# Products of the substitution in other buffers, more turns for the projections, four HGRN tiles moved forward, and all low parts of weights on DVE

## The chip, the cores and the metric

The kernel runs on one core of a Trainium2 chip. The metric is the time of one execution in microseconds (us), taken on the device; the median of several runs counts. The engines of the core are named as in the profile: PE (matrix products; its weight loads are PEld), DVE (vector), ACT (scalar, activation functions), POOL (general) and SP, which issues most of the transfers.

## The reference

One decoder layer on 512 tokens of width 2048, in float32. Two groups of heads share one input projection, and a mixer of single-neuron experts (PEER) follows.

```
xn = rmsnorm(x);  proj = xn @ w_in            # 57 column tiles of 128
o_a = hgrn2(a_q, a_f, a_i)                    # 8 heads: S_t = diag(f_t) S_{t-1} + (1-f_t) v_t ; o_t = S_t^T q_t
qkv = silu(causal_conv(b_q|b_k|b_v));  q, k l2-normalised
o_b = gated_delta(q, k, v, beta, g)           # 8 heads on 4 q/k pairs; chunkwise:
      M = I + strict_lower(kb k^T * L);  u, w = M^-1 (v beta), M^-1 (kb exp(g))
h = x + concat(gated_norm(o_a), gated_norm(o_b)) @ w_out
hn = rmsnorm(h);  scores = hn @ w_query @ sub_keys;  top-16 of each, top-16 of sums -> experts, gates
y_t = sum_e gate_e * gelu(u_e . hn_t) * v_e   # 16384 experts
out = rmsnorm(h + y)
```

## The kernel before

**Weights.** Every weight goes through `wunit`: SP loads a raw tile of 128x1024 (`wr`), ACT casts it to the short format (`wh`, L100), and the difference of the two, the low part (`wl`, L102), is made by POOL, or by DVE where the call says so. Each of the three has three buffers. A projection step (`mm3`, L239 to L241) is then three products: high weight with high and low activation, low weight with high activation. Sixteen steps fill one column tile. 114 units belong to the input projection, 32 to the output projection, 32 to PEER's queries: their low parts are on POOL. The 512 units of the expert tables have theirs on DVE.

**Front.** The input is normalised and split into high and low (`front`, L742). Then the projection stream (`proj_steps`, L210) and the heads run interleaved: a chain of a head is a generator, and at each of its `yield`s the loop `run` (L253) gives the stream a number of turns, 1.8 in the GDN pairs (RATE_B) and 5.0 in the HGRN heads (RATE_A). A turn is one step, three products. The stream stops short where two tiles of the coming kind are still unused. `jobs` (L722) lists the column tiles in order: the gates, then what the four pairs need, then forget, query, value and gate tile of each HGRN head.

**A pair.** `gdn_pair` (L402) makes the keys' Gram matrix (L420), two matrices to be inverted, and sends their 32x32 diagonal blocks through memory. `substitute` (L482) inverts these blocks row by row on DVE: 31 steps, each a product into a buffer `m` (L498) and a sum into `T_` (L500), with a `yield` after every fourth. The results return through memory, and `inverse` (L512) joins them to 128x128 by small products on PE (L527, L533, L542), whose copies go to the buffers `iTN` and `iY`. Beside the substitution the queries are normalised (`unit_q`, `l2n`): a square on ACT into a buffer `t_sq` (L376), a product with ones on PE (L380). `m` is taken from the same two `t_sq` buffers. L442 is the product of q and k; the chains of the two heads follow.

**A head.** `hgrn_head` (L605) needs its forget and query tile first, then goes through seven levels, each some products on PE (L624, L631) and some work on DVE (L587, L638, L639), then states (L653) and output (L666).

**Then** the output projection (`wout_steps`), PEER's scores with top-16 on DVE (`scores`, `top16`, L956 to L970), and the experts, which take the rest of the time.

**Order.** A scheduler puts the instructions of each engine in an order when the kernel is built; each engine works off its own queue in that order. So the places below are those of the built program.

Of the kernel before, what the change touches and what calls it, by code (L numbers as in the profile page):

```python
# [33 lines left out]
IB = 32  # L34
# [43 lines left out]
class Kernel:  # L78
# [12 lines left out]
        return (pool or self.fp).tile(list(shape), dt, tag=tag, name=self.nm(tag), bufs=bufs)  # L91


    def wunit(self, src, raw=False, eng=None):
        nc, wp = self.nc, self.wp
        full = raw
        raw = wp.tile([P, 8, P], F32, tag="wr", name=self.nm("wr"))
        nc.sync.dma_start(raw, src)
        hi = wp.tile([P, 8, P], F32R, tag="wh", name=self.nm("wh"))
        nc.scalar.copy(hi, raw)  # L100
        lo = wp.tile([P, 8, P], F32R, tag="wl", name=self.nm("wl"))
        (eng or nc.gpsimd).tensor_tensor(lo, raw, hi.bitcast(F32), op=ALU.subtract)  # L102
        return (raw, hi, lo) if full else (hi, lo)

    def linear(self, src, halves, xh, xl, ps):
# [376 lines left out]
    def substitute(self):  # L482


        nc = self.nc
        TT = self.TT
        nb = self.ft("iN", (P, IB, IB))
        T_ = self.ft("iT", (P, 8, IB))
        nc.sync.dma_start(T_, self.a["eye"])
        yield  # L490
        for g in range(IG):
            nc.sync.dma_start(nb[g * NX:(g + 1) * NX], self.nd.rearrange("j h c s t -> (j h c) s t"))
        for _ in range(WAIT):
            yield
        for s in range(IB - 1):
            w = IB - 1 - s
            m = self.ft("t_sq", bufs=2)[:, 0:8 * IB].rearrange("p (j i) -> p j i", j=8)[:, :, 0:w]
            nc.vector.tensor_tensor(m, nb[:, s:s + 1, s + 1:].to_broadcast([P, 8, w]),  # L498
                                    T_[:, :, s:s + 1].to_broadcast([P, 8, w]), op=ALU.mult)
            nc.vector.tensor_tensor(T_[:, :, s + 1:], T_[:, :, s + 1:], m, op=ALU.add)  # L500
            if s % 4 == 3:
                yield
        for g in range(IG):
            nc.sync.dma_start(self.td.rearrange("j h c s t -> (j h c) s t")[:, 8 * g:8 * g + 8],
                              T_[g * NX:(g + 1) * NX])
        for j in range(P // IB):
            sl = slice(j * IB, (j + 1) * IB)
            nc.sync.dma_start(TT[sl, :, :, sl], self.td[j].rearrange("h c s t -> s h c t"))
        for _ in range(WAIT):
            yield  # L510
# [211 lines left out]
    def jobs(self):  # L722

        key = lambda j: (36 + j, lambda ps: self.conv_silu(ps, 4 + j, "gk"), "k")
        out = [(56, self.gates, "gates")]
        for j in range(4):
            if j == 0:
# [2 lines left out]
            for h in (2 * j, 2 * j + 1):  # L730
                if j < 3 and h % 2:
                    out.append(key(j + 1))
                out.append((40 + h, lambda ps, h=h: self.conv_silu(ps, 8 + h, "gv"), "v"))
                out.append((48 + h, self.gate, "u"))
        for h in range(8):
            out.append((8 + h, lambda ps, h=h: self.forget(ps, h), "f"))
            out.append((h, lambda ps: self.keep(ps, "hQ"), "r"))
            out.append((16 + h, lambda ps: self.keep(ps, "gv"), "v"))
            out.append((24 + h, self.gate, "u"))
        return out  # L740
# [366 lines left out]
    def u_steps(self, et):  # L1107
# [1 line left out]
        nc = self.nc  # L1109
        ps = self.pt("lin")[:, 0:TD]  # L1110
        for h in (0, 1):
            hi, lo = self.wunit(self.a["u"][et][h], eng=nc.vector)
            for k in range(8):
                self.mm3(ps, hi[:, k], lo[:, k], 8 * h + k, k + h == 0, 8 * h + k == KT - 1)
            if h == 0:
# [35 lines left out]
    def v_chunk(self, g, dc, w, last):  # L1151

        nc = self.nc
        wh, wl = w
        hi, lo = self.wunit(self.a["v"][g, dc].rearrange("p (x y) -> p x y", x=8), eng=nc.vector)
        hv, lv = (x.rearrange("p (e z) n -> p e (z n)", e=4) for x in (hi, lo))
        for dd in range(2):
            dt = 2 * dc + dd
# [187 lines left out]
```

## Time and profile before

| | |
|---|---|
| median of 3 runs | 3533.93 us (3527.35 to 3548.31) |
| profiled execution | 3537.38 us, span 3534.2 us |
| granted PE clock, mean | 0.966 |
| busy: PE, DVE, ACT, POOL | 3323.9, 2760.3, 1206.8, 878.8 us |
| start to the gates (0 to 65 us) | PE busy 42.3 us, clock 0.91 |
| four GDN pairs (65 to 541 us) | PE busy 428.3 of 475.6 us, clock 0.88 |
| HGRN heads (541 to 951 us) | PE busy 403.5 of 410.0 us, clock 1.00 |
| output projection and scores (951 to 1353 us) | PE busy 384.8 of 402.2 us |
| the rest (experts) | PE busy 2065.1 of 2181 us |

In rows of the profile, `wl<-wr,wh` means that tile wl is written from wr and wh, L102 is the line, and `x54` the number of instructions. A time in brackets at a row's end, as `[6.94 <-ACT t_sq L376]`, is how long the engine had been idle before, and what ended that. In a table of waits the numbers are the total in us, how many, and the longest. A window row gives its bounds and length in us, the busy times, then the granted clock, the busy share of the transfer engines and GB/s.

### The profile page before, as it was taken

What the parts mean: (1) busy time and instruction counts of PE and PEld (TensorE: products, weight loads), DVE (VectorE), ACT (ScalarE), POOL (GpSimd) and SP (SyncE); (2) the same over time, 40 slices, a digit from 0 to 9 for tenths busy, and PEclk for the clock granted to TensorE, in tenths of its full rate; (3) what the DMA queues carried; (4) which work ended last, traced back from release to release, by engine and by line L of the source; (5) the groups of instructions that cost most, each with busy time, mean ns of one, the idle gap of its engine ahead of it and who ended that gap; (6) DMA issues with size and microseconds to landing.
All of it is one profiled execution on the core that took longest, in us unless ns stands there. A gap on an engine that the chain in (4) does not pass through costs nothing.

```text
span 3534.2 us, 49832 instructions
## 1 busy us (share of the span) xinstructions
PE 3323.9 (94%) x19740; PEld 3085.3 (87%) x19740; DVE 2760.3 (78%) x4095; ACT 1206.8 (34%) x1499; POOL 878.8 (25%) x533
## 2 busy tenths in 40 slices
PE   7889899999999997898999799999999998999997
PEld 5667678888788896898989799999999998999997
DVE  7675654444534679998999799998999998999966
ACT  5333433322332212343435233332333334333334
POOL 4232223333354231011121222222222222111100
PEclk9899989999999998999999999999999999999999
DMA  4232222222442223677788899999999999999963
GB/s 147 76 96 88 83 64 81 78 81 78 130 130 85 71 66 120 209 293 292 277 318 294 316 346 375 370 368 355 358 360 365 372 366 333 349 322 335 332 183 111
DMA packets 238028, 801.63 MB, mean 227 GB/s; under 512 B 30202, under 2 KB 99066, under 8 KB 194978
## 3 DMA queue, kind: packets, MB, share of 16 engines
q1 hardware_dynamic: 191714, 462.88, 37.9%
q0 software_dynamic: 46080, 335.56, 25.2%
q8 instruction: 154, 2.52, 0.3%
q14 instruction: 80, 0.66, 0.1%
HBM read 754.50 MB, written 43.86 MB: 226 GB/s over the span
## 4 chain that ended last, share of the span: by engine, by line
PE 51%; DVE 19%; issue 14%; DMA 12%; POOL 2%; ACT 1%; SPq 0%; DVEq 0%; POOLq 0%; ACTq 0%
PE lin L239 8%; PE lin L241 7%; PE lin L240 7%; DMA row<-vn,eidx 3%; DVE wl L102 3%; DMA wr<-u 3%; PE g L1165 2%; PE g L1164 2%; PE g L1163 2%; POOL row L1205 2%; PE lin L1165 2%; PE lin L1164 2%; PE lin L1163 2%; DVE row L1218 2%; DMA wr<-v 1%
## 5 line engine op out<-in xcount | busy, mean ns | idle before, releaser
L100 ACT CAST wh<-wr 128x1024 fp32r<-128x1024 f32 x690 | 724.5, 1050 | 1708.8 <-DMA wr<-v 402.3
L241 PE MATMUL lin<-yh,wl 128*128 128x352 f32 x2048 | 673.0, 329 | 68.5 <-DVE wl L102 68.2
L102 DVE TENSOR_TENSOR wl<-wr,wh 128x1024 fp32r<-128x1024 f32 x512 | 623.3, 1219 | 81.6 <-ACT wh L100 80.3
L239 PE MATMUL lin<-yh,wh 128*128 128x352 f32 x2048 | 673.3, 329 | 9.5 <-ACT wh L100 9.5
L240 PE MATMUL lin<-yl,wh 128*128 128x352 f32 x2048 | 668.0, 326 | 0.0
L102 POOL TENSOR_TENSOR wl<-wr,wh 128x1024 fp32r<-128x1024 f32 x178 | 432.8, 2432 | 872.8 <-ACT wh L100 809.8
L241 PEld LDWEIGHTS lin<-yh,wl 128*128 128x128 f32 x2048 | 391.3, 191 | 78.8 <-DVE wl L102 78.4
L1205 POOL DMA_INDIRECT row<-un,eidx x160 | 212.4, 1328 | 809.7 <-DVE row L1218 626.2
L239 PEld LDWEIGHTS lin<-yh,wh 128*128 128x128 f32 x2048 | 391.7, 191 | 11.3 <-ACT wh L100 11.3
L1205 POOL DMA_INDIRECT row<-vn,eidx x160 | 201.2, 1258 | 782.8 <-DVE y_nat L1231 416.0
L240 PEld LDWEIGHTS lin<-yl,wh 128*128 128x128 f32 x2048 | 391.1, 191 | 0.0
L239 PE MATMUL lin<-xh,wh 128*128 128x512 f32 x912 | 381.4, 418 | 8.9 <-ACT xh L766 8.8
L1165 PE MATMUL g<-wgh,wl 128*128 128x352 f32 x1188 | 384.9, 324 | 3.5 <-DVE wl L102 3.3
L1164 PE MATMUL g<-wgl,wh 128*128 128x352 f32 x1188 | 385.4, 324 | 0.0
L1163 PE MATMUL g<-wgh,wh 128*128 128x352 f32 x1188 | 382.4, 322 | 2.3 <-ACT wh L100 2.3
L240 PE MATMUL lin<-xl,wh 128*128 128x512 f32 x912 | 375.5, 412 | 2.5 <-DVE xl L767 2.3
L241 PE MATMUL lin<-xh,wl 128*128 128x512 f32 x912 | 373.0, 409 | 4.4 <-POOL wl L102 4.4
L1231 DVE SCALAR_TENSOR_TENSOR y_nat<-row,ww,y_nat 128x2048 f32<-128x2048 f32 x128 | 300.3, 2346 | 11.1 <-DMA row<-vn,eidx 10.7
L1218 DVE SCALAR_TENSOR_TENSOR row<-row,hn_nat 128x2048 f32<-128x2048 f32 x128 | 292.1, 2284 | 1.7 <-DMA row<-un,eidx 1.5
L1165 PEld LDWEIGHTS g<-wgh,wl 128*128 128x128 f32 x1188 | 223.3, 188 | 5.5 <-DVE wl L102 5.4
L1163 PEld LDWEIGHTS g<-wgh,wh 128*128 128x128 f32 x1188 | 223.5, 188 | 2.6 <-ACT wh L100 2.6
L1164 PEld LDWEIGHTS g<-wgl,wh 128*128 128x128 f32 x1188 | 223.2, 188 | 0.0
(348 smaller groups left out, 5879.5 us busy)
## 6 DMA issues: line engine op xcount, KB each, us to landing
wr<-u SPq DMA_DIRECT2D x256, 512.0 KB, 6.2
wr<-v SPq DMA_DIRECT2D x256, 512.0 KB, 6.7
wr<-wi SPq DMA_DIRECT2D x114, 512.0 KB, 3.6
gd<-st SPq DMA_DIRECT2D x11, 2048.0 KB, 13.6
gm<-gd SPq DMA_DIRECT2D x32, 704.0 KB, 9.3
wr<-wo SPq DMA_DIRECT2D x32, 512.0 KB, 3.6
wr<-wq SPq DMA_DIRECT2D x32, 512.0 KB, 3.5
hidd<-hid SPq DMA_DIRECT2D x64, 176.0 KB, 5.2
```

The costliest lines, as they stand in the source:

```text
L100: nc.scalar.copy(hi, raw)
L102: (eng or nc.gpsimd).tensor_tensor(lo, raw, hi.bitcast(F32), op=ALU.subtract)
L239: mm(ps, hi, self.xh[:, k], start=first, stop=False)
L240: mm(ps, hi, self.xl[:, k], start=False, stop=False)
L241: mm(ps, lo, self.xh[:, k], start=False, stop=last)
L1163: nc.tensor.matmul(ps, hv[:, e, sl], wh[:, e], start=(e == 0), stop=False)
L1164: nc.tensor.matmul(ps, hv[:, e, sl], wl[:, e], start=False, stop=False)
L1165: nc.tensor.matmul(ps, lv[:, e, sl], wh[:, e], start=False, stop=(e == 3))
L1205: ins = nc.gpsimd.indirect_dma_start(out=r, out_offset=None, in_=self.a[tab], in_offset=bass.IndirectOffsetOnAxis(ap=idx, axis=0))
L1218: nc.vector.scalar_tensor_tensor(r, r, 1.0, hn, op0=ALU.mult, op1=ALU.mult, accum_out=ww[:, i:i + 1])
L1231: nc.vector.scalar_tensor_tensor(y, r, ww[:, i:i + 1], y, op0=ALU.mult, op1=ALU.add)
```

## The change

Four edits. The products `m` of the substitution go in turn to the buffers `iTN` and `iY`, which the inverse uses later. The substitution yields after every second step in place of every fourth. Four tiles of the heads 0 and 1 (forget 0, query 0, forget 1, query 1) are taken into the list of jobs among the tiles of the four pairs. And `wunit` makes every low part on DVE, 178 of them that were on POOL.

```diff
--- before.py
+++ after.py
@@ -91,7 +91,7 @@
         return (pool or self.fp).tile(list(shape), dt, tag=tag, name=self.nm(tag), bufs=bufs)
 
 
-    def wunit(self, src, raw=False, eng=None):
+    def wunit(self, src, raw=False):
         nc, wp = self.nc, self.wp
         full = raw
         raw = wp.tile([P, 8, P], F32, tag="wr", name=self.nm("wr"))
@@ -99,7 +99,7 @@
         hi = wp.tile([P, 8, P], F32R, tag="wh", name=self.nm("wh"))
         nc.scalar.copy(hi, raw)
         lo = wp.tile([P, 8, P], F32R, tag="wl", name=self.nm("wl"))
-        (eng or nc.gpsimd).tensor_tensor(lo, raw, hi.bitcast(F32), op=ALU.subtract)
+        nc.vector.tensor_tensor(lo, raw, hi.bitcast(F32), op=ALU.subtract)
         return (raw, hi, lo) if full else (hi, lo)
 
     def linear(self, src, halves, xh, xl, ps):
@@ -494,11 +494,11 @@
             yield
         for s in range(IB - 1):
             w = IB - 1 - s
-            m = self.ft("t_sq", bufs=2)[:, 0:8 * IB].rearrange("p (j i) -> p j i", j=8)[:, :, 0:w]
+            m = self.ft(("iTN", "iY")[s % 2])[:, 0:8 * IB].rearrange("p (j i) -> p j i", j=8)[:, :, 0:w]
             nc.vector.tensor_tensor(m, nb[:, s:s + 1, s + 1:].to_broadcast([P, 8, w]),
                                     T_[:, :, s:s + 1].to_broadcast([P, 8, w]), op=ALU.mult)
             nc.vector.tensor_tensor(T_[:, :, s + 1:], T_[:, :, s + 1:], m, op=ALU.add)
-            if s % 4 == 3:
+            if s % 2:
                 yield
         for g in range(IG):
             nc.sync.dma_start(self.td.rearrange("j h c s t -> (j h c) s t")[:, 8 * g:8 * g + 8],
@@ -722,6 +722,8 @@
     def jobs(self):
 
         key = lambda j: (36 + j, lambda ps: self.conv_silu(ps, 4 + j, "gk"), "k")
+        forget = lambda h: (8 + h, lambda ps: self.forget(ps, h), "f")
+        query = lambda h: (h, lambda ps: self.keep(ps, "hQ"), "r")
         out = [(56, self.gates, "gates")]
         for j in range(4):
             if j == 0:
@@ -732,9 +734,11 @@
                     out.append(key(j + 1))
                 out.append((40 + h, lambda ps, h=h: self.conv_silu(ps, 8 + h, "gv"), "v"))
                 out.append((48 + h, self.gate, "u"))
+
+            out.append(forget(j // 2) if j % 2 == 0 else query(j // 2))
         for h in range(8):
-            out.append((8 + h, lambda ps, h=h: self.forget(ps, h), "f"))
-            out.append((h, lambda ps: self.keep(ps, "hQ"), "r"))
+            if h >= 2:
+                out += [forget(h), query(h)]
             out.append((16 + h, lambda ps: self.keep(ps, "gv"), "v"))
             out.append((24 + h, self.gate, "u"))
         return out
@@ -1109,7 +1113,7 @@
         nc = self.nc
         ps = self.pt("lin")[:, 0:TD]
         for h in (0, 1):
-            hi, lo = self.wunit(self.a["u"][et][h], eng=nc.vector)
+            hi, lo = self.wunit(self.a["u"][et][h])
             for k in range(8):
                 self.mm3(ps, hi[:, k], lo[:, k], 8 * h + k, k + h == 0, 8 * h + k == KT - 1)
             if h == 0:
@@ -1152,7 +1156,7 @@
 
         nc = self.nc
         wh, wl = w
-        hi, lo = self.wunit(self.a["v"][g, dc].rearrange("p (x y) -> p x y", x=8), eng=nc.vector)
+        hi, lo = self.wunit(self.a["v"][g, dc].rearrange("p (x y) -> p x y", x=8))
         hv, lv = (x.rearrange("p (e z) n -> p e (z n)", e=4) for x in (hi, lo))
         for dd in range(2):
             dt = 2 * dc + dd
```

The scheduler answers with another order. On DVE, where the substitution of pair 0 begins, before; in the names, `t_sq` is a product's buffer, `iT` the sum, `gv` and `t_u` tiles of the stream:

```order
L364 SCALAR_TENSOR_TENSOR t_y_586<-pad_583,sm,t_y_586 128x512 x3
L359 MEMSET pad_1033 128x3
L369 SCALAR_TENSOR_TENSOR gv_593<-t_th_591,t_y_586 128x512
L498 TENSOR_TENSOR t_sq_605<-iN_531,iT_532 128x8x31
L500 TENSOR_TENSOR iT_532<-iT_532,t_sq_605 128x8x31
L498 TENSOR_TENSOR t_sq_608<-iN_531,iT_532 128x8x30
```

and after:

```order
L383 SCALAR_TENSOR_TENSOR gq_507<-gq_507,t_r_690 128x512
L245 TENSOR_TENSOR t_u_714<-lin_595,rstd_a 128x512
L102 TENSOR_TENSOR wl_849<-wr_845,wh_847 128x1024
L498 TENSOR_TENSOR iTN_605<-iN_531,iT_532 128x8x31
L444 TENSOR_TENSOR geg_389<-gq_507,geg_389 128x512
L500 TENSOR_TENSOR iT_532<-iT_532,iTN_605 128x8x31
L285 SCALAR_TENSOR_TENSOR t_u_714<-t_th_713,t_u_714 128x512
L498 TENSOR_TENSOR iY_608<-iN_531,iT_532 128x8x30
```

A low part now stands directly ahead of the first step, the products alternate between two other buffers, and the normalised query (L383) is finished before the substitution begins.

On ACT, around the square of pair 0's query (`t_sq<-gq`), before:

```order
L100 CAST wh_977<-wr_975 128x1024
L100 CAST wh_1052<-wr_1050 128x1024
L367 ACTIVATE t_th_899<-t_y_894 128x512
L376 ACTIVATE t_sq_686<-gq_507 128x512
L100 CAST wh_1098<-wr_1096 128x1024
```

and after:

```order
L150 ACT_TABLE_LOAD
L376 ACTIVATE t_sq_656<-gq_507 128x512
L100 CAST wh_727<-wr_725 128x1024
L367 ACT_TABLE_LOAD
L367 ACTIVATE t_th_591<-t_y_586 128x512
```

The square stood behind the tanh of the tile that DVE works off during the substitution (the key tile, `t_y_894`); now it stands ahead of the tanh of the tile before (`t_y_586`), which is worked off before the substitution begins.

On PE, at the states of the first HGRN head (`lin` is the stream's tile), before:

```order
L241 MATMUL lin_4233<-xh,wl_4238 128x512
L653 MATMUL g_4275<-gTn_4253,gN_4246 128x128 x3
L239 MATMUL lin_4233<-xh,wh_4236 128x512
L240 MATMUL lin_4233<-xl,wh_4236 128x512
L241 MATMUL lin_4233<-xh,wl_4238 128x512
L239 MATMUL lin_4233<-xh,wh_4290 128x512
```

and after:

```order
L239 MATMUL lin_4454<-xh,wh_4497 128x512
L653 MATMUL g_4313<-gTn_4306,gN_4299 128x128 x3
L666 MATMUL o_4323<-gL_4133,gTn_4306 128x128 x2
L240 MATMUL lin_4454<-xl,wh_4497 128x512
L241 MATMUL lin_4454<-xh,wl_4499 128x512
```

Between the states and the head's output stood 15 products of the stream; now none does.

## The prediction

> **What bounds the kernel now.** I read the busy times by stage first, then the waits of the stage that the change touches, then the order of events around each wait. The rows of stages give, for a stretch in us, its length and the busy time of PE, PE's weight loads, DVE, ACT and POOL, then the granted clock.
>
> ```profile
> 65.20:540.80 475.60, 428.29 (x2197) 335.15 (x2196) 293.25 (x598) 182.06 (x251) 131.39 (x54) 0.88 0.28 83
> 540.80:639.20 98.40, 96.88 (x533) 81.05 (x532) 44.91 (x87) 28.53 (x33) 32.60 (x14) 1.00 0.26 81
> 1075.00:1353.00 278.00, 261.98 (x1624) 250.82 (x1622) 176.69 (x772) 55.19 (x67) 92.11 (x42) 0.98 0.24 76
> ```
>
> The first row is the four GDN pairs: PE is idle for 47.3 of 475.6 us and its clock is 0.88. The second is HGRN heads 0 and 1: PE is full, at full clock, and DVE works less than half the time. The third is the query scores, where DVE is at 177 of 278 us. So PE's stream of projection products (lines 239 to 241, "projections" below) sets the time of the front, except in the pairs, where something else holds PE up. Within a pair two stretches matter: from the product of the keys (L420) to the first transpose of the inverse (L527), here called the window, and from there to the product of q and k (L442), here the block.
>
> ```profile
> 73.60:136.40 62.80, 54.25 (x230) 43.50 (x229) 57.76 (x104) 27.55 (x31) 22.56 (x10) 0.92 0.33 92
> 424.70:489.30 64.60, 55.57 (x234) 44.40 (x232) 44.57 (x91) 25.01 (x29) 23.41 (x10) 0.92 0.31 92
> sum 256.40, PE 217.40 PEld 174.08 DVE 200.80 ACT 97.85 POOL 92.26; mean PE 54.35 PEld 43.52 DVE 50.20 ACT 24.46 POOL 23.06
> ```
> ```profile
> 136.40:156.00 19.60, 19.60 (x142) 13.91 (x142) 3.25 (x11) 4.29 (x8) 3.98 (x2) 0.55 0.09 28
> 257.80:278.70 20.90, 20.90 (x142) 14.84 (x142) 2.56 (x10) 3.65 (x7) 2.36 (x1) 0.50 0.15 50
> 379.50:392.80 13.30, 13.30 (x148) 9.74 (x148) 8.05 (x17) 6.53 (x10) 2.36 (x1) 1.00 0.30 91
> 489.30:509.90 20.60, 20.60 (x143) 14.53 (x143) 2.56 (x10) 3.65 (x7) 2.39 (x2) 0.51 0.09 27
> ```
>
> The first and the last of the four windows, their sum, and the four blocks. The windows hold 39 us of PE's idle time. Three of the four blocks ran at about half the clock. What PE waits for, in total, times and longest:
>
> ```profile
> PE g L380 <- ACT t_sq L376: 30.2, 4, 9.1
> ACT t_sq L376 <- DVE iT L500: 11.9, 2, 6.1
> PE g L527 <- DMA gT<-gTd: 6.5, 3, 3.1
> ```
> ```profile
> 117.61 0.63 ACT L367 ACTIVATE t_th<-t_y 128x512 f32<-128x512 f32 x1 [10.04 <-DVE t_y L364]
> 118.14 0.61 ACT L376 ACTIVATE t_sq<-gq 128x512 f32<-128x512 f32 x1
> 118.81 2.08 PE L380 MATMUL g<-t_sq,fc 128*128 128x512 f32 x2 [6.94 <-ACT t_sq L376]
> ```
>
> Once per pair PE stops at the norm of q (L380), 30.2 us in all. It waits for the square on ACT (L376). In two pairs that square waits for a t_sq buffer that the substitution's products hold (L500); in the pair shown it stands on ACT behind a tanh that waits for a convolution that DVE works off between the substitution's steps. Then DVE and POOL:
>
> ```profile
> 95.80 0.41 DVE L500 TENSOR_TENSOR iT<-iT,t_sq 128x240 f32<-128x240 f32 x1
> 97.17 2.25 DVE L500 TENSOR_TENSOR iT<-iT,t_sq 128x232 f32<-128x232 f32 x1
> 96.77 2.40 POOL L102 TENSOR_TENSOR wl<-wr,wh 128x1024 fp32r<-128x1024 f32 x1 [2.17 <-ACT wh L100]
> ```
> ```profile
> L102 DVE TENSOR_TENSOR wl<-wr,wh x512: 1194/1218/1281, 1347.2 to 3504.0; 128x1024 fp32r<-128x1024 f32 x171
> L102 POOL TENSOR_TENSOR wl<-wr,wh x54: 2337/2392/2912, 73.6 to 540.0; 128x1024 fp32r<-128x1024 f32 x54
> ```
> ```profile
> L100 ACT CAST wh<-wr 128x1024 fp32r<-128x1024 f32 x690 | 724.5, 1050 | 1708.8 <-DMA wr<-v 402.3
> ```
>
> A smaller step of the substitution took 2.25 us in place of 0.41 because a low part ran on POOL, and it ended just behind it. The low part itself takes 2.39 us (median) on POOL and 1.22 us on DVE; the cast ahead of it takes 1.05 us on ACT.
>
> **Prices.** A projection costs 0.228 us: twelve starts in 2.74 us.
>
> ```profile
> 821.33 0.40 PE L241 MATMUL lin<-xh,wl 128*128 128x512 f32 x1
> ...
> 824.07 0.40 PE L241 MATMUL lin<-xh,wl 128*128 128x512 f32 x1
> ```
>
> **The turns and the four tiles.** The order of instructions gives the number of projections in each stretch. Windows: 217, 218, 209, 220 before (864), 258, 254, 254, 235 after (1001). Blocks: 93 and 93. Rest of the pairs: 336 and 363. Heads 0 and 1: 326 and 156; from there the counts are alike. So 170 projections, 38.8 us of PE's work, leave the heads, where PE is full; 137 of them go into the windows and 27 into the rest (6 more before the pairs). Those in the rest I price in full, +6 us. Whether those in the windows are free depends on how long a window becomes.
>
> **The windows.** Three pieces, from the rows of the substitution:
>
> ```profile
> 92.38:128.84 36.46, 15.41 (x31) 0.86 0.24 75
> sum 139.94, DVE 48.83; mean DVE 12.21
> sum 139.94, DVE 56.96; mean DVE 14.24
> L498 DVE TENSOR_TENSOR t_sq<-iN,iT x124: 162/292/2561, 92.4 to 479.2; 128x248 f32<-128x248 f32 x4, 128x240 f32<-128x240 f32 x4, 128x232 f32<-128x232 f32 x4, 128x224 f32<-128x224 f32 x4
> 77.41 2.33 DVE L364 SCALAR_TENSOR_TENSOR t_y<-pad,sm,t_y 128x512 f32<-128x512 f32 x3
> ```
>
> The first row is pair 0's substitution with its L498 instructions; the two sums are L498's and L500's busy time in all four, 105.8 us in 139.9 us. At L498's median, which I take for L500 too, the 248 instructions would need 72.5 us: POOL stretches them by 33 us. Without POOL that is gone, but 23 low parts now stand between the steps (28 us), and the tails of two and a half more tiles (two more convolutions, 2.33 us and three single passes each, 8.6 us in all). So the substitutions grow by some 3 us. Ahead of them, pair 0's window takes 18.8 us (92.4 less 73.6), all four 84.6; after, the last low part ahead of the first step needs PE to be 69, 65, 65 and 70 projections past the keys, which with L380 (2.1 us), a cast and a low part for each comes to 79 us: -6. Behind them the way through memory to L527 stays at 7.6 us, -1 in pair 3. Sum, with the overlap of neighbouring instructions on DVE rounded off, -5: 251 us. Bounds: PE's own work there, 1001 x 0.228 + 4 x 2.1 = 237 us (-19), and +12, if each low part in the windows holds DVE up for half a us more.
>
> That the square no longer waits follows from its place: ahead of the substitution, in buffers that nothing else holds. The products themselves cost what they did: iTN and iY are next written by the inverse's copies (L528, L537), behind the last step. The 30 us of L380 are therefore not a term of their own; the 137 projections (31 us) fill them. What is late next is L527: after, the last low part of a substitution needs PE within 45 projections of L527 (10.3 us), while cast, low part, last steps and the way through memory need about 11 us. PE will again wait for L527, by about 1 us.
>
> **The blocks.** At full clock such a block takes 13.3 us with 27 projections, 12.2 with 22; the three slow ones lost 61.1 - 36.6 = 24.5 us. They stood behind the three waits for L527; the fourth, with no wait, ran at 1.00. With waits of about 1 us, between none and the shortest that slowed a block, I take half: -12 (0 to -24.5).
> By the Trainium skill (TensorE: Matmul & The Clock Gate, section "Why this matters for your kernels") the clock falls back after an idle gap of about 3 us or more. The row of the three waits differs: 6.5 us in all, the longest 3.1, and each followed by a slow block, so shorter waits did it too; the measurement decides. By the rule shorter waits would save nothing here, and the sum would end 12 us higher.
>
> **The start.**
>
> ```profile
> 33.49 11.61 DVE L776 TENSOR_TENSOR t_acc<-t_acc,t_sq 128x512 f32<-128x512 f32 x7
> 36.24 8.32 POOL L102 TENSOR_TENSOR wl<-wr,wh 128x1024 fp32r<-128x1024 f32 x3
> 46.13 2.07 PE L137 MATMUL o<-t_sq,fc 128*128 128x512 f32 x2 [3.44 <-DVE t_sq L779]
> ```
>
> Three low parts on POOL stretch the seven last sums of squares, on which the first norm waits. After, these three stand on DVE behind the sums, but three others ahead of them (3.7 us). I take -5 of 8.3 us (0 to -9).
>
> **Heads 0 and 1.** PE's work falls to 98.4 - 38.8 = 59.6 us. A level needs its chain through DVE:
>
> ```profile
> 656.45 1.00 PE L624 MATMUL g<-hQ,hK 128*128 128x64 f32 x8
> 657.49 0.44 DVE L587 COPY_PREDICATED gL<-mk,g 128x256 f32<-128x256 uint8 x1 [3.01 <-PE g L624]
> 658.16 0.42 DVE L639 TENSOR_TENSOR hK<-hK,hf 128x256 f32<-128x256 f32 x1
> ```
>
> That is 2.1 us from a level's products to what the next ones need; with the 1.00 us of the products and 6 to 9 projections between (1.4 to 2.1 us), PE is just covered. Behind L653 no projection is left ahead of L666. New idle time +5 (0 to +14): -34 in all.
>
> **Output projection and scores.** 64 low parts add 78 us to DVE, which has room (177 of 278 us in the scores).
>
> ```profile
> PE g L959 <- DVE t_y L956: 15.8, 7, 2.4
> ```
>
> PE already waits for an odd tile's scores, behind the top-16 work. The next tile's low part now stands directly behind that instruction: at most 1.2 us more for 8 tiles, less what POOL stretched. +2 (-8 to +10).
>
> Sum: -5 -5 -12 +6 -34 +2 = -48. The profiled execution took 3537.4 us (its span and 3.2 around it), 3.5 above the median of 3533.9: the median becomes 3486. The PEER stages keep their instructions; SP issues as many loads, each now released by DVE's reading of the raw weights where it was POOL's; POOL keeps its squares at the start, its 16 scalings and its gathers.
>
> **Rivals.**
> First, PE sets the windows: DVE stays ahead, they shrink to 237 us (-14 more) and L527 finds its data, so that all blocks run at full clock (-12 more): 3460. For it: DVE overlaps successive instructions, which my sum ignores; pair 2 had no wait. Against: the 45 projections above.
> Second, the low parts hold DVE. DVE takes its queue in order, so a low part that waits for its cast holds every step behind it.
>
> ```profile
>   ACT wh L100: 286.7, 45
> ```
>
> POOL waited for casts 45 times in the pairs, 6.4 us each, at nobody's cost. If each of 61 low parts there costs 0.4 us of PE's time, 3510. Against: the order sets each where its cast is due.
> By the Trainium skill (TensorE: Matmul & The Clock Gate, its opening table) the queues of ScalarE and VectorE are strict FIFO; the trace agrees, L376 above starting only as L367 ends.
> Third, the turns are only moved: heads 0 and 1, bare of projections, take as long as before, because their chain is what lasts: 3486 + 34 = 3520, about no change. Against: the 2.1 us of a level.
> Fourth, slower: in the scores PE runs out of low parts behind each odd tile's 44 DVE instructions, two thirds of a tile pair's 22 us (177 by 8), so some 15 us. Were all of that, less the 2.2 us it waits now, a wait on each of the 8 odd tiles, 3486 + 8 x 12.8 = 3588; it decides from 8 us a tile on. Against: both units of the odd tile stand ahead of that run.
>
> **Chances.** My sum 0.54 (3470 to 3502), first rival 0.20, second 0.16, third 0.06, fourth 0.04. About 0.5% (18 us) is what a measurement of this kernel tells from no change. Faster by more: 0.54 + 0.20 + most of the second, 0.85; within: 0.11; slower 0.04. The range reaches from beyond the first rival to the third: 3452 to 3519.
>
> **What would show it.** No wait of PE for L376; DVE steps of the substitution without any near 2.4 us; 1001 projections in windows of about 251 us; PE at L527 waiting about 1 us and the clock of the blocks; heads 0 and 1 in some 65 us; scores at 278 us. I am wrong if low parts on DVE show long waits for ACT, or if PE in the pairs waits for them.

## The result, and the profile after

The changed kernel takes 3431.53 us (median of 4 runs, 3425.67 to 3437.62), against 3533.8 us before: a ratio of 0.9715, interval 0.9686 to 0.9745. On a second chip it took 3439.49 against 3526.95 us: 0.9747, 0.9721 to 0.9773. The forecast was 3486, range 3452 to 3519: the sign was right, the gain was twice what was forecast, and the time lies below the range. The profiled execution took 3437.6 us, its span is 3435.8.

The three stages that the prediction began with (bounds and length in us, then busy PE, weight loads, DVE, ACT, POOL, then the granted clock): the pairs, heads 0 and 1, the scores. The prediction's row for the scores, 278.0 us from 1075, also held 39 us of the output projection; the last row here is the kernel before from the first product of the scores on, to be set beside the third.

```profile
55.74:478.30 422.56, 420.07 (x2362) 336.60 (x2362) 295.30 (x665) 190.81 (x261) 0.00 (x0) 1.00 0.34 102
478.30:537.90 59.60, 59.54 (x363) 48.20 (x362) 39.17 (x88) 19.43 (x24) 0.00 (x0) 1.00 0.23 71
1007.50:1256.00 248.50, 231.54 (x1468) 225.45 (x1467) 187.09 (x792) 44.48 (x50) 2.47 (x2) 0.95 0.24 73
...
1113.90:1355.10 241.20, 225.18 (x1466) 220.54 (x1465) 167.28 (x762) 43.78 (x50) 72.93 (x32) 0.97 0.24 76
```

In the pairs PE was idle for 47.3 us at a clock of 0.88; now it is idle for 2.5 us at 1.00, though it does 164 projections more there. POOL does nothing at all in the pairs. The first and last window (keys to first transpose) with the sum of all four, then the four blocks (first transpose to the product of q and k):

```profile
66.09:126.48 60.39, 60.39 (x270) 49.52 (x268) 48.40 (x109) 28.20 (x32) 0.00 (x0) 1.00 0.38 103
...
378.38:435.09 56.71, 55.71 (x248) 45.46 (x247) 42.58 (x96) 23.80 (x27) 0.00 (x0) 1.00 0.36 105
sum 237.13, PE 235.62 PEld 192.79 DVE 188.03 ACT 103.36 POOL 0.00; mean PE 58.90 PEld 48.20 DVE 47.01 ACT 25.84 POOL 0.00
```
```profile
126.48:139.08 12.60, 12.60 (x145) 9.14 (x145) 5.95 (x16) 4.20 (x8) 0.00 (x0) 1.00 0.33 97
231.17:243.33 12.16, 12.16 (x144) 8.77 (x143) 3.72 (x11) 3.66 (x7) 0.00 (x0) 1.00 0.33 99
335.42:348.27 12.85, 12.85 (x147) 9.32 (x146) 7.63 (x18) 4.20 (x8) 0.00 (x0) 1.00 0.35 99
435.09:447.23 12.14, 12.14 (x143) 8.77 (x142) 3.72 (x11) 3.66 (x7) 0.00 (x0) 1.00 0.32 91
```

The windows are as long as PE's own work, and all four blocks run at full clock. The steps of the substitution, product and sum, by group (count, then busy us and mean ns), and the wait of PE with the largest sum between the gates and the experts:

```profile
L498 DVE TENSOR_TENSOR iTN<-iN,iT 128x248 f32<-128x248 f32 (+7 forms) x64 | 18.6, 291 | 1.4
L500 DVE TENSOR_TENSOR iT<-iT,iTN 128x248 f32<-128x248 f32 (+7 forms) x64 | 18.6, 290 | 1.5
L498 DVE TENSOR_TENSOR iY<-iN,iT 128x240 f32<-128x240 f32 (+14 forms) x60 | 17.4, 290 | 1.4
L500 DVE TENSOR_TENSOR iT<-iT,iY 128x240 f32<-128x240 f32 (+14 forms) x60 | 17.4, 290 | 1.4
```
```profile
PE g L963 <- DVE t_y L960: 15.1, 8, 2.1
```

The 248 steps take 72.0 us, where they took 105.8. Piece by piece, in the two profiled executions (us):

| piece | before | after | change | forecast |
|---|---|---|---|---|
| start to the gates | 65.2 | 55.7 | -9.4 | -5 |
| four windows | 256.3 | 237.1 | -19.2 | -5 |
| four blocks | 74.4 | 49.7 | -24.7 | -12 |
| rest of the pairs | 144.9 | 135.7 | -9.2 | +6 |
| heads 0 and 1 | 98.4 | 59.6 | -38.8 | -34 |
| heads 2 to 7 | 322.0 | 317.3 | -4.7 | 0 |
| output projection and scores | 394.0 | 400.8 | +6.8 | +2 |
| experts | 2179.1 | 2179.8 | +0.7 | 0 |

### The profile page after: what moved, and what is told of

It is laid out like the page before. It is cut to its first block, busy times and chain, and to the rows that moved or that the text cites. A ratio compares the mean times of both kernels' runs of the same rounds, so it can differ in the third digit from the quotient of the medians.

```text
span 3435.8 us, 49785 instructions
## 1 busy us (share of the span) xinstructions
PE 3281.1 (95%) x19740; PEld 3056.3 (89%) x19740; DVE 2795.4 (81%) x4273; ACT 1205.8 (35%) x1498; POOL 449.7 (13%) x355
## 4 chain that ended last, share of the span: by engine, by line
PE 48%; DVE 21%; issue 15%; DMA 13%; POOL 2%; ACT 1%; DVEq 0%; SPq 0%; POOLq 0%; ACTq 0%
PE lin L239 8%; PE lin L241 8%; PE lin L240 8%; DVE wl L102 5%; DMA wr<-u 4%; DMA wr<-v 3%; DVE row L1222 3%; DMA row<-vn,eidx 2%; DVE hT L1170 2%; DVE y_nat L1235 2%; POOL row L1209 2%; PE g L1169 2%; PE g L1168 1%; PE g L1167 1%; PE lin L115 1%
## 5 line engine op out<-in xcount | busy, mean ns | idle before, releaser
L102 DVE TENSOR_TENSOR wl<-wr,wh 128x1024 fp32r<-128x1024 f32 x690 | 840.3, 1219 | 240.3 <-ACT wh L100 236.8
L239 PE MATMUL lin<-xh,wh 128*128 128x512 f32 x912 | 371.5, 408 | 9.1 <-ACT xh L770 8.9
L240 PE MATMUL lin<-xl,wh 128*128 128x512 f32 x912 | 362.4, 398 | 1.3 <-DVE xl L771 1.3
L241 PE MATMUL lin<-xh,wl 128*128 128x512 f32 x912 | 362.9, 398 | 0.3 <-DVE wl L102 0.3
L1209 POOL DMA_INDIRECT row<-un,eidx x160 | 203.9, 1274 | 1051.7 <-DVE row L1222 633.3
L239 PEld LDWEIGHTS lin<-xh,wh 128*128 128x128 f32 x912 | 172.7, 189 | 42.8 <-ACT xh L770 8.9
```

What stands on the lines that cost most here:

```text
L102: nc.vector.tensor_tensor(lo, raw, hi.bitcast(F32), op=ALU.subtract)
L239: mm(ps, hi, self.xh[:, k], start=first, stop=False)
L240: mm(ps, hi, self.xl[:, k], start=False, stop=False)
L241: mm(ps, lo, self.xh[:, k], start=False, stop=last)
L1209: ins = nc.gpsimd.indirect_dma_start(out=r, out_offset=None, in_=self.a[tab], in_offset=bass.IndirectOffsetOnAxis(ap=idx, axis=0))
```

## The experiments

They ran on three chips, on which the kernel before took 3536.8, 3535.2 and 3527.0 us. The experts, which the change leaves alone, differ by 9 to 10 us between two profiled executions of the same kernel. The end of the front (the first product of the output projection, L113) is steadier: 855.2 and 854.2 us in two executions of the changed kernel. So the last column is the one to read. A is the products' buffers, B the turns, C the four tiles, D the low parts; "idle" is PE's idle time in the windows, "slow" the blocks at a granted clock of 0.75 or less.

| kernel | median | ratio to before | windows (idle) | blocks (slow) | rest | L113 |
|---|---|---|---|---|---|---|
| before | | | 256.3 (39.0) | 74.4 (3) | 144.9 | 961.2 |
| D alone | 3451.87 | 0.9767 (0.9740 to 0.9793) | 226.7 (2.7) | 49.1 (1) | 138.2 | 863.6 |
| A alone | 3550.06 | 1.0044 (1.0022 to 1.0065) | 255.1 (52.1) | 81.9 (4) | 151.4 | 976.2 |
| A, D | 3448.03 | 0.9776 (0.9748 to 0.9805) | 221.5 (2.6) | 48.2 (0) | 139.2 | 858.3 |
| A, B, C (D undone) | 3560.14 | 1.0065 (1.0042 to 1.0088) | 258.0 (49.5) | 83.8 (4) | 173.2 | 980.6 |
| B, C, D (A undone) | 3438.85 | 0.9717 (0.9679 to 0.9754) | 236.7 (2.5) | 49.9 (0) | 134.6 | 854.7 |
| A, C, D (B undone) | 3453.73 | 0.9777 (0.9725 to 0.9828) | 236.6 (4.4) | 56.5 (1) | 141.2 | 868.9 |
| A, B, D (C undone) | 3455.09 | 0.9760 (0.9719 to 0.9802) | 230.2 (8.7) | 50.1 (1) | 142.0 | 870.5 |
| all four, again | 3439.49 | 0.9747 (0.9721 to 0.9773) | 237.6 (1.9) | 49.8 (0) | 135.2 | 854.2 |
| all, low parts made twice | 3505.02 | 0.9909 (0.9884 to 0.9935) | 268.3 (28.5) | 67.7 (2) | 148.7 | 923.3 |
| all, late substitutions | 3452.66 | 0.9796 (0.9761 to 0.9830) | 245.8 (4.0) | 55.3 (1) | 139.3 | 870.2 |
| all, sums of scores spread | 3422.93 | 0.9709 (0.9682 to 0.9735) | 237.3 (1.6) | 49.7 (0) | 135.8 | 853.7 |

**The low parts back on POOL (D undone).**

```diff
-        nc.vector.tensor_tensor(lo, raw, hi.bitcast(F32), op=ALU.subtract)
+        (eng or nc.gpsimd).tensor_tensor(lo, raw, hi.bitcast(F32), op=ALU.subtract)
 ...                                             # and eng=nc.vector again for the expert tables
```

> The changed kernel with the 178 low parts of the projections and queries back on POOL. The order gives windows of 216, 232, 225 and 210 projections (883 in place of 1001). Theory one (cover): steps of 2.3 us come back in the substitution, the windows last about 62 us each as they did before (250 in all) while PE has 210 us of work in them, so some 35 to 40 us of idle time return; three or four blocks fall to half clock (18 to 25 us); the start loses its 9.4 us: +62 to +74, 3494 to 3506. Rival (the buffers of the products and the fill carry the gain; POOL's stretching is hidden as long as PE has projections): +9 for the start and at most 15 in the windows, 3441 to 3456.

It went further than either theory: 3560.14 us, slower than the kernel before. The four windows (first, last, sum), the wait, and one of the four blocks:

```profile
73.56:137.02 63.46, 50.98 (x229) 41.67 (x227) 57.89 (x103) 24.83 (x29) 23.83 (x10) 0.93 0.31 90
...
463.32:525.08 61.76, 49.83 (x224) 40.71 (x222) 46.51 (x85) 22.58 (x26) 22.65 (x9) 0.94 0.29 86
sum 257.96, PE 208.44 PEld 170.38 DVE 213.53 ACT 95.69 POOL 96.42; mean PE 52.11 PEld 42.59 DVE 53.38 ACT 23.92 POOL 24.11
```
```profile
PE g L527 <- DMA gT<-gTd: 49.5, 4, 14.0
```
```profile
268.24:289.19 20.95, 20.95 (x142) 14.84 (x142) 2.56 (x10) 4.94 (x8) 1.90 (x1) 0.50 0.08 27
```

With A, PE does not stop at L380 any more; it stops at L527 instead, for 49.5 us where the two stops together were 36.7 us before, and all four blocks run at half clock. The stream that runs on past L380 also brings more of POOL's low parts into the substitutions: 23 where 17 overlapped them before. What went beyond theory one lies behind the windows and blocks: the rest of the pairs takes 37.5 us more than in the changed kernel and heads 0 and 1 take 16.4 us more, in part because the 118 projections that the windows lost (27 us) are done there.

**D alone, and A with D.**

```diff
 # the kernel before, with
-        (eng or nc.gpsimd).tensor_tensor(lo, raw, hi.bitcast(F32), op=ALU.subtract)
+        nc.vector.tensor_tensor(lo, raw, hi.bitcast(F32), op=ALU.subtract)
 # and, for the second kernel, also
-            m = self.ft("t_sq", bufs=2)[...]
+            m = self.ft(("iTN", "iY")[s % 2])[...]
```

> The kernel before with one edit alone: all low parts on DVE. The order gives windows of 245, 242, 248 and 213 projections (948), and L380 158 to 186 projections behind the keys. Theory one: with steps of 0.41 us the t_sq buffers come free in time, L380 does not wait, the first three windows are as long as PE's work (57 us), the last one waits for L527 as in the run without the four tiles; 3450 to 3470, that is 70 to 85 of the 102 us. Rival, the blind sum's (a square that stands behind the substitution's tiles keeps PE waiting, whoever makes the low parts): half of L380's 30 us stay, and blocks run at half clock: 3480 to 3500.

> The kernel before with the products in iTN and iY and all low parts on DVE; turns and tiles as before. The order gives windows of 258, 237, 231 and 204 projections (930). Theory one (with D, the buffers of the products carry nothing): the same as with D alone within 8 us, 3450 to 3470. Rival (A frees the square, D the steps, each half of the gain): 15 to 30 us less than D alone.

D alone has 97.6 of the 106 us that the front gained; A on top of it brings 5 (863.6 to 858.2 us), and the medians, 3451.87 and 3449.70 us on the chip that ran both, do not tell the two apart. The rival's 30 us at L380 are gone with D alone: L380 stands 158 to 186 projections behind the keys, the square still in the old buffers, and PE waits 0.7 us for it, once. One thing in it no theory had: the fourth block ran at 0.63 without a wait ahead of it. By the order only 3 projections stand in it, where 22 or 23 stand in the others, and PE is idle for 2.9 us inside it:

```profile
425.23:437.70 12.47, 9.61 (x125) 8.18 (x124) 3.79 (x11) 3.65 (x7) 0.00 (x0) 0.63 0.29 85
```

**A alone.** The edit is the second half of the diff above, on the kernel before.

> The kernel before with one edit alone: the products in iTN and iY. The order moves L380 from 155 to 164 projections behind the keys to 76 to 86, so PE no longer waits there (30 us before). Theory one (the window is as long as DVE's stretched chain): the same time comes back as a wait for L527 (7 to 9 us a pair more), all four blocks at half clock: 3530 to 3550, no gain. Rival (the wait for the square is a cost of its own): 20 to 30 us faster, 3505 to 3515.

The wait moved, and grew. In the list of waits L380 is gone, and in its place stands

```profile
PE g L527 <- DMA gT<-gTd: 52.1, 4, 16.1
```

The kernel is 0.44% slower. POOL's low parts that overlap the substitutions are 24, and the steps take 120.3 us. Over the three kernels with POOL each such low part costs DVE about 2 us beyond the 72.0 us of free steps: (105.8 - 72.0) / 17, (113.8 - 72.0) / 23 and (120.3 - 72.0) / 24 are 2.0, 1.8 and 2.0.

**A undone.**

```diff
-            m = self.ft(("iTN", "iY")[s % 2])[...]
+            m = self.ft("t_sq", bufs=2)[...]
```

> The changed kernel, with the substitution's products back in the two t_sq buffers. By the order the four windows hold 991 projections (1001 in the changed kernel), and the norm of q (L380) stands 124 to 144 projections behind the keys, where it stood 57 to 76. Theory one (the gain is one of cover: from the keys to the inverse PE never runs out, so no gap forms and the clock stays up): a square that waits for a t_sq buffer stops PE at L380 again; as before that is 2 pairs by 6 us or so, and the stretch behind such a stop runs at half clock; +12 to +30 us, 3444 to 3462. Rival, DVE's freedom from POOL is all (theory two): the buffers come free every 0.4 us when no step is stretched, so the square waits one step at most; +0 to +5, 3431 to 3437.

The rival was right: the front ends at 854.7 us, as in the changed kernel, and nothing waits at L380.

**Low parts made twice.** This tells POOL's presence from the order in which DVE has its work. PE's and DVE's queues are the changed kernel's.

```diff
         nc.vector.tensor_tensor(lo, raw, hi.bitcast(F32), op=ALU.subtract)
+        if twice:                                  # the first 19 column tiles
+            for k in range(0, 8, 2):
+                x = wp.tile([P, 2, P], F32, tag="wx", ..., bufs=1)
+                nc.gpsimd.tensor_tensor(x, raw[:, k:k + 2], hi.bitcast(F32)[:, k:k + 2], op=ALU.subtract)
```

> The changed kernel, but POOL makes the low parts of the first 19 column tiles a second time, a quarter at a time, into a tile that nobody reads; DVE's own low parts stay and PE uses those. The order of PE and of DVE is the changed kernel's to the row (1001 projections in the windows). Theory one (POOL's work at DVE's side is what stretches the substitution): steps of 2 us and more come back, DVE's low parts are stretched as well, PE waits for L527 in all four pairs by some 8 to 14 us and the blocks fall to half clock: +60 to +110 us, 3490 to 3540. Rival (what the edit gained is the order and the place of the low parts, ahead of the step that can wait): the extra work is read by nobody, +0 to +15 us, 3431 to 3447.

The 19 tiles end with pair 1, not with pair 3 as I had reckoned, so the run holds its own control. The windows, then the blocks; the second last busy column is ACT, the last is POOL:

```profile
77.16:152.50 75.34, 62.67 (x270) 50.52 (x269) 65.27 (x109) 27.75 (x32) 43.23 (x44) 0.94 0.28 82
212.12:287.40 75.28, 61.32 (x266) 49.75 (x265) 63.62 (x107) 24.73 (x29) 37.44 (x40) 0.93 0.30 88
343.18:403.91 60.73, 60.07 (x267) 49.04 (x266) 49.20 (x110) 26.29 (x31) 0.00 (x0) 1.00 0.37 106
446.53:503.43 56.90, 55.72 (x249) 45.47 (x247) 42.77 (x96) 23.82 (x27) 0.00 (x0) 1.00 0.35 105
```
```profile
152.50:174.29 21.79, 21.79 (x145) 15.48 (x145) 7.78 (x16) 4.26 (x8) 4.08 (x4) 0.50 0.21 59
287.40:308.33 20.93, 20.93 (x143) 14.82 (x143) 3.79 (x11) 3.65 (x7) 3.90 (x4) 0.50 0.21 61
403.91:416.74 12.83, 12.83 (x145) 9.32 (x145) 7.63 (x18) 4.20 (x8) 0.00 (x0) 1.00 0.34 99
503.43:515.58 12.15, 12.15 (x143) 8.76 (x142) 3.72 (x11) 3.66 (x7) 0.00 (x0) 1.00 0.29 90
```

Work that nobody reads costs 69 us in the front (923.3 against 854.2), 15 us in each of the two windows beside which it runs and 9 us in the block behind each; pairs 2 and 3 are the changed kernel's to half a us. The steps themselves, with POOL beside them:

```profile
98.82 3.63 POOL L106 TENSOR_TENSOR wx<-wr,wh 128x256 f32<-128x256 f32 x3
...
99.75 0.95 DVE L502 TENSOR_TENSOR iTN<-iN,iT 128x248 f32<-128x248 f32 x1
...
101.77 0.95 DVE L504 TENSOR_TENSOR iT<-iT,iTN 128x248 f32<-128x248 f32 x1
...
107.08 0.40 DVE L504 TENSOR_TENSOR iT<-iT,iTN 128x232 f32<-128x232 f32 x1
```

A step beside POOL's quarter (0.99 us on average) lasts 0.95 us; beside a whole low part of 2.40 us it lasted 2.25. A stretched step lasts about as long as the instruction on POOL; a free one 0.40. The Trainium skill (SBUF — State Buffer, section "SBUF: two separate sides") says why: DVE with two inputs in the buffer memory and POOL share a pair of ports, and one holds it for the whole instruction while the other stands still. Both rows agree.

**B undone, C undone.**

```diff
-            if s % 2:                    # B undone
+            if s % 4 == 3:
-            out.append(forget(j // 2) if j % 2 == 0 else query(j // 2))    # C undone
-            if h >= 2:
-                out += [forget(h), query(h)]
+            out += [forget(h), query(h)]
```

> The changed kernel with a turn only after every fourth step of the substitution. The order gives windows of 258, 249, 251 and 228 projections, 986 in all in place of 1001, and the blocks as they are. Theory one (cover): 15 projections, 3.4 us, are missing in the windows, less than would let a gap of over 1 us form in any one of them except perhaps the last (7 fewer, 1.6 us); 0 to +8 us, one block at half clock at most: 3431 to 3440. Rival (the turns carry the fill): the windows lose their cover at the end, all four blocks fall to half clock: +25 us or more, 3456 and up.

> The changed kernel with the forget and query tiles of heads 0 and 1 back in their old place. The order gives windows of 258, 255, 243 and 182 projections (938 in place of 1001), and 81 projections fewer ahead of the first head. Theory one (cover): the first two windows stay as they are; in the fourth PE runs 53 projections (12 us) short, waits for L527 for about that time and its block falls to half clock (7 us); heads 0 and 1 get back 81 projections, 18.5 us, that fill no gap there: about +20 us, 3450. Rival (the window is as long as DVE's chain, and that shrinks with the tiles' own convolutions): the fourth window shrinks by those 12 us with the work, no wait, clock full: +0 to +5 us, 3433.

Both came out slower in the front, by 14.7 and 16.3 us. C's theory held in kind: 7.67 us of waiting in pair 3 in place of the 12 I gave, half clock behind it (in a block that has lost all its projections, which by the row of D alone lowers the clock too), and 17.6 us back in heads 0 and 1; the fourth window shrank by 5 us, which is the rival's direction. B's did not hold in its size, 14.7 us where it had at most 8. By its rival all blocks would have fallen; one did. The three waits of PE for the inverse, the issues of the transfers in ahead of the first, and the blocks behind the first two:

```profile
229.14 0.40 PE L527 MATMUL g<-fc,gT 32*32 32x32 f32 x8 [1.31 <-DMA gT<-gTd]
...
343.97 0.39 PE L527 MATMUL g<-fc,gT 32*32 32x32 f32 x8 [1.10 <-DMA gT<-gTd]
...
445.46 0.39 PE L527 MATMUL g<-fc,gT 32*32 32x32 f32 x8 [1.09 <-DMA gT<-gTd]
```
```profile
224.58 0.37 SPq L98 DMA_DIRECT2D wr<-wi  x1
225.75 1.80 SPq L508 DMA_DIRECT2D gT<-gTd  x4
```
```profile
229.14:248.85 19.71, 19.71 (x144) 14.12 (x144) 3.70 (x11) 3.65 (x7) 0.00 (x0) 0.56 0.15 47
343.97:356.08 12.11, 12.11 (x142) 8.75 (x143) 3.35 (x12) 3.66 (x7) 0.00 (x0) 1.00 0.17 51
```

The block behind 1.31 us of waiting took 7.5 us more, the one behind 1.10 us nothing more. These waits do not come from the 15 missing projections alone. In each of the three pairs SP issues a weight load 1.1 to 1.2 us ahead of the transfers in, and by the trace's records of landing the first of these lands 3.0 to 3.4 us behind its issue; in the changed kernel no load stands there, and it takes 1.6 to 1.8 us. Without B and C both (A and D alone) the front ends at 858.3 us, better than with only one of them undone: the two fit each other, and what they bring beyond A and D is 3 to 4 us in the front.

**Late substitutions.** A delay, with no POOL near:

```diff
+        for _ in range(LATE.pop(0)):               # 4, 8, 6, 16 in the four pairs
+            nc.vector.tensor_scalar(T_, T_, 1.0, None, op0=ALU.mult)
         for g in range(IG):
             nc.sync.dma_start(self.td...             # the way through memory
```

> The changed kernel, with passes of DVE that multiply the finished substitution by one ahead of its way through memory: 4, 8, 6 and 16 in the four pairs, about 0.35 us each. By the order PE has 7 and 21 projections more in the first two windows, which cover that, 1 less and 1 more in the last two (253 and 236 in place of 254 and 235), which don't. Theory one (a short wait ahead of the block costs the block its clock): no wait and blocks of 12 to 13 us in the first two pairs; waits of 1.5 to 2 and of 4.5 to 5.5 us in the last two, and blocks of 19 to 21 us there: +20 to +24 us in the front. Rival (the block is slow for what POOL or the substitution do beside it, not for the wait): the blocks stay at 12 to 13 us, +6 to +8 us.

The passes took 0.29 us, and the scheduler put fewer tails of tiles on DVE in the last two pairs, so the waits came out shorter: 0.62 and 0.20 us in the first two pairs, 1.23 in the third, 1.59 in the fourth. The edit also moved the loads: in all four pairs one now stands just ahead of the transfers in, whose first lands 3.1 to 4.1 us behind its issue. So the waits come from the passes and from these loads together. The blocks of the last two:

```profile
346.62:359.18 12.56, 12.56 (x145) 9.13 (x145) 4.66 (x13) 3.66 (x7) 0.00 (x0) 1.00 0.13 43
447.75:466.19 18.44, 17.71 (x136) 12.66 (x136) 3.70 (x11) 3.66 (x7) 0.00 (x0) 0.52 0.07 26
```

Theory one holds for the fourth pair, at a third of the expected wait, and not for the third, whose 1.23 us cost nothing. So a block is slow without POOL too. The two blocks differ in their projections as well, 24 and 16; the cleaner pair is the second block of the run with B undone (23 projections, 1.31 us, 19.7 us) and that of the changed kernel (22, none, 12.2).

**The changed kernel again, and A with D beside it.** No edits.

> The changed kernel once more, on the chip of the next three. In the profiles it and the kernel with A and D alone differ by 3 us up to the output projection (855.2 and 858.1 us), but by 18 us in the medians (3431.5 and 3449.7), which were taken at different times. Theory one (turns and tiles bring little once D is there, and the medians differ by the chip's own spread): 3437 to 3445 here, within 6 us of the kernel with A and D. Rival (turns and tiles together bring 18 us): 3428 to 3435.

> The kernel with A and D alone (products in iTN and iY, low parts on DVE; turns and tiles as before), once more beside the changed kernel. Theory one: 3443 to 3450, within 6 us of the changed kernel. Rival: 15 to 20 us behind it.

3439.49 and 3448.03 us: 8.5 us apart, between the two theories, with runs that overlap (3431.8 to 3444.2 and 3433.3 to 3453.2). By the front it is 4 us. That B and C bring something is likely, its size is not settled; D, with A or without, is 2.2 to 2.3% of the 2.5 to 2.9%.

**The sums of scores spread.** A version that beats the changed kernel too:

```diff
+                        heads = []
                         for n in range(16):
                             self.scores(n)
                             if n % 2:
-                                for c in range(NC_):
-                                    self.top_head(c, n // 2)
+                                heads += [(c, n // 2) for c in range(NC_)]
+                            while len(heads) > (2 if n % 2 else 0) or n == 15 and heads:
+                                self.top_head(*heads.pop(0))
 ...                                             # and two instructions kept in program order
```

> The changed kernel, with the top-16 of pairs of scores spread in the query scores: of the four that follow an odd tile, two are done behind that tile and two behind the next even one, and the order of these sums and of the scaled queries (L960) is fixed as written. In the changed kernel PE waits 2.1 us for L960 seven times, and about 3.4 us at half clock follow each time. By the order no more than one low part now stands between such a sum's work and L960. Theory one (cover): the waits fall below 1 us and the half clock behind them goes: 7 x (1.1 to 2.1) + 7 x 1.7 = 20 to 27 us faster than the changed kernel. Rival (the wait is the time from a tile's last product through L960 back to PE, whatever stands ahead): the waits stay near 2 us, within 5 us of the changed kernel.

3422.93 us, 16.6 less than the changed kernel on the same chip. The scores there, and the waits that take the place of L963's:

```profile
1006.10:1233.10 227.00, 220.33 (x1471) 214.51 (x1470) 195.71 (x792) 44.05 (x50) 2.47 (x2) 1.00 0.25 82
```
```profile
PE g L965 <- DVE t_y L962: 6.3, 13, 0.6
```

The stage lasts 227.0 us where it lasted 247.3 beside it: thirteen waits of half a us in place of seven of 2.1, and the clock at 1.00 where it was 0.96. Theory one's 20 us came in the stage; the medians show 16.6 of them. How much of it the fixed order alone would bring, without the spreading, no run tells.

## Why the prediction was wrong, point by point

**Right in kind.** Heads 0 and 1 fell to 59.6 us, PE's own work, as counted; the second, third and fourth rival are out. DVE did wait for casts in the pairs, 15 times for 22.4 us, and PE was not held up by it. The price of POOL was right: 33 us of stretching, measured 33.8. The wait for the square went, as said. The scores grew by a little, 7.3 us from their first product on, and no low part starved PE there: its waits for low parts in them were 0.3 us at the longest.

**The windows (-5, measured -19.2): the step that failed is the length of the chain ahead of L527, DVE's part and the way through memory.** The sum was -6 ahead of the first step, +3 for the substitutions and -1 for the way back, made -5 for the overlap; measured were -2.4, -8.7 and -8.0. From first step to last the substitutions took 139.9 us before and 131.2 after, where I had 143. The steps themselves were right (72.0 us). But all other instructions there grew by 33 us, not by 37, their overlap with their neighbours by 3 us (their lengths add up to 136.3 us, DVE is busy for 123.8), and DVE's idle time fell by 5 us. The overlap, which the prediction named and then only rounded off, is thus a quarter of this miss of 12 us. The way back, from the last step to L527, was taken as fixed at 7.6 us; it took 6.5, 5.7, 4.9 and 6.6. The transfers of pair 0, before and after, then the last step and L527 after:

```profile
131.83 0.35 SPq L98 DMA_DIRECT2D wr<-wi  x1
132.73 1.79 SPq L508 DMA_DIRECT2D gT<-gTd  x4
```
```profile
119.30 0.33 SPq L98 DMA_DIRECT2D wr<-wi  x1
...
119.81 0.18 DVE L500 TENSOR_TENSOR iT<-iT,iTN 128x8 f32<-128x8 f32 x1
120.02 1.72 SPq L504 DMA_DIRECT2D gTd<-iT  x4
123.89 1.79 SPq L508 DMA_DIRECT2D gT<-gTd  x4
...
126.48 0.40 PE L527 MATMUL g<-fc,gT 32*32 32x32 f32 x8
```

Before, a weight load stood 0.9 us ahead of the transfers in, and by the trace's records of landing the first of these landed 3.5 us behind its issue, at 136.25; after, the last load lies 4.6 us back, and it took 1.7 us, landing at 125.60. PE takes it at 126.48: covered, by 0.9 us. So the wait of 1 us that I set at L527 never came. The same holds in all pairs, 3.3 to 4.0 us before and 1.6 to 1.8 after, and in all 56 of the fourteen profiled executions: 2.8 to 4.1 us where a load was issued 0.5 to 1.5 us ahead (25 pairs), 1.6 to 1.8 us where the last load lay more than 4 us back (31 pairs). The prediction did not ask where SP's loads fall, and no run moved them by themselves.

**The blocks (-12, measured -24.7): half was the wrong share.** With no wait there is no lost clock. This follows from the step above, but the step was poor by itself: a single block mostly loses all or nothing. In the ten profiled executions with no low part on POOL, 34 of the 35 blocks behind no wait or one up to 1.23 us ran at full clock (the other is the one with 3 projections), and the two behind 1.59 and 7.67 us at half; between them 1.31 us did cost the clock, 1.40 and 1.54 us did not. What the prediction says the cited rule would give can be read the other way too: a rule that lets a wait of 1 us pass leaves the blocks at full clock, and the sum would end 12 us lower, not higher.

**The rest of the pairs (+6, measured -9.2): priced as work alone.** It holds 27 projections more, 6.2 us, as counted. But in the kernel before PE was idle there for 8.3 us, and parts of it ran at a lower clock: the first stretch, behind the start, at 0.71, and those behind the three slow blocks at 0.94 to 0.96. The first two stretches and the sum:

```profile
65.18:73.61 8.43, 8.43 (x32) 6.47 (x31) 2.19 (x10) 5.19 (x6) 0.00 (x0) 0.71 0.51 178
156.02:190.46 34.44, 32.22 (x173) 25.52 (x173) 18.74 (x40) 15.31 (x26) 7.14 (x4) 0.96 0.29 92
...
sum 144.88, PE 136.57 PEld 108.21 DVE 76.05 ACT 66.16 POOL 28.04; mean PE 27.32 PEld 21.64 DVE 15.21 ACT 13.23 POOL 5.61
```

After, 1.0 us of idle time and a clock of 1.00 are left. A stage that was not in the list of changed things changed because its neighbours did.

**The small terms.** The start gave its full bound of 9 where I took 5. The 5 us of new idle time in the heads did not come: 0.06 us. These two, the windows, the blocks and the rest are 51 us together; the profiled executions differ from the sum by 50.

**The first rival** (PE sets the windows at 237 us, blocks at full clock) is what happened, to a tenth of a us in the windows. I gave it 0.20 and priced it 3460, because it kept my +6 for the rest, the small start and the idle time of the heads. What it lacked is that most of these hang together: the windows, the blocks, the rest and the heads all have PE covered, and when DVE keeps ahead of PE their losses go at once (the start is apart). The range ended at 3452, 8 us beyond this rival. With the start, the windows, the blocks and the heads all at their lower bounds and the other two terms as given, the sum is 3451; most of the 20 us from there to 3431.5 is the rest of the pairs, 15 us below its term, which had no bound.

**What I had not asked** is which of the four edits carries the gain. The prediction made A and the new place of the square carry the end of L380's wait, and B and C the filling of it. D alone did nearly all, and A, B and C without D cost 23 us.

## What to carry to other kernels

When one engine's work stretches another's, price that first: moving work from POOL to a DVE that was already the busier of the two made the kernel faster, since each low part on POOL had cost DVE's chain 2 us and took DVE 1.2. A wait that is removed comes back at the next place unless the chain behind it got shorter, as A alone showed; look at what the freed engine runs into next. Look also at what stands ahead of a short transfer on which a chain waits: here those issued just behind a weight load landed 1 to 2.4 us later than the others. And terms that share one condition, here that PE never runs out, should be given as one case with one chance, at all their bounds together.

## What the runs showed of the hardware

The clock drops for waits far shorter than I had taken from the rows of before: ahead of a stretch of small products every wait of 1.59 us or more cost it, 1.31 us did once, 1.40 and 1.54 us did not. Products of 32 and 64 columns do not bring it back: the clock stays at half to the block's end or beyond, for 20.5 to 34.1 us by the records of the granted clock, which come in steps of 3.41 us (the longest begin within the wait). (The one exception is the third block of the run with A alone, which holds 29 projections and ends at full clock.) Projections in the block seem to help to keep it, as the block with 3 of them suggests. A wait of 2.1 us among products of 160 and 352 columns (L963) is followed by one such step of 3.4 us only.

The Trainium skill (TensorE: Matmul & The Clock Gate, section "What's actually happening") gives a window of about 3.4 us that runs freely, and half clock after an idle one. The traces bear out the first: in each of the fourteen profiled executions all changes of the clock lie on one grid of 3.41 us, to 0.01 us over the whole span, whatever the waits do. That a whole window must be idle does not agree with 1.59 us. Laid on that grid, 22 of its windows begin at full clock and hold more than 1 us of a wait for L527. In the 16 that ended in half clock, at most 5 products of 512 columns start; in the 6 that kept it, 6 to 8. Of the wait of 1.31 us, 1.06 us lie in a window with 5; those of 1.40 and 1.54 us lie in windows with 6 and 7. So the work of PE in the window tells the two kinds apart here, where the length of the wait does not. What work is enough in a window without such a wait is not shown, and no run varied the phase by itself.
